# Paired loads, a regrouped triangular inverse and a new order table in phase two of a bidirectional RWKV-7 layer

## The chip, the cores and the metric

The kernel runs on one core of a Trainium2 chip. The metric is the device time of one execution in microseconds, taken as the median of several runs. The engines are named as in the profile: PE (TensorE, matmuls), ACT (ScalarE), DVE (VectorE), POOL (GpSimd) and SP (SyncE, which here only issues DMA transfers).

## What is computed

One layer of a bidirectional RWKV-7 trunk over 4096 + 512 tokens of width 1024 with 16 heads of 64: norm, input projection, a delta rule recurrence run forward and backward over the tokens, a group norm, gate, output projection and a last norm. The recurrence is what phase two of the kernel computes:

```python
def step(s, inp):
    r_t, w_t, k_t, v_t, kk_t, a_t = inp
    sa = jnp.einsum("bhvk,bhk->bhv", s, -kk_t)
    s = (s * w_t[:, :, None, :]
         + sa[..., None] * (kk_t * a_t)[:, :, None, :]
         + v_t[..., None] * k_t[:, :, None, :])
    return s, jnp.einsum("bhvk,bhk->bhv", s, r_t)
...
y_fwd = delta_rule_scan(r_h, heads(decay[:, :, 0]), ...)
y_bwd = flip(delta_rule_scan(flip(r_h), flip(heads(decay[:, :, 1])), ...))
y = y_fwd + y_bwd
```

## The kernel before

There are three phases: the input projection (to about 2000 us of the trace), the recurrence (to about 4290 us) and the output projection. The change touches the second alone.

Phase two does the recurrence in chunks of 64 tokens. A double step D covers 256 tokens of each direction (`tok` gives the first token: the forward direction goes up, the backward one down) for two pairs of heads, the halves `hf` 0 and 1, called lanes. There are 4 x 18 = 72 double steps. Each is cut into about 230 named steps. In a name the first figure is the half; in the names of four characters a second figure counts the chunk `i`.

- Loads, all on SP's queue, each issued in program order: `lk`, `lb`, `lr` (tiles `k`, `kb`, `r`, one transfer of 128 x 256 for each direction), `lt` (tile `ta`, L554, two transfers, one for each direction, each with both low-rank inputs x = 0 and 1), `uv` (values), `wa` (weights of the low-rank products, every 18th double step).
- Stage A: `lw` and `la` (L571, low-rank products of x = 0 and x = 1 on PE; both read `ta` and write `z`), tanh steps `tw`, `tW`, `ta`, `tA` on ACT, `pl`, the scan `sn` on DVE, exponentials `e1`, `e2`, then the elementwise steps `bf`, `al`, `kf`, `rh`, `kb`, `kk` on DVE (capital second letter: backward direction) with `fc` on ACT, scores `s0` to `s7` on PE with masks `m0` to `m3` on DVE, transposes `x0`, `x1` on PE with copies `c0`, `c1` on ACT.
- Triangular inverse of the 32 x 32 blocks: `ga` writes masked scores out to DRAM (eight transfers), `gw` and `gb` read them back as `w` and `lt`, then fifteen parts `E0` to `E14` (L783) run one after the other on the same tile `w`. Part b has the columns j = 2b+1 and 2b+2, each a product `tm` (or `td` on DVE) and an addition, of ceil(j/2) x (31-j) elements. `ON_DVE = (6, 12)` puts two parts on DVE, the others run on POOL. `ms` sets the diagonal on POOL, `S1` and `S2` move the result by DRAM into `xt`.
- Stage B: `xr`, `g0`, `g1`, `gc`, `gC`, `h0`, `h1`, `hc`, `hC` complete the inverse.
- Chain, four chunks for each lane: on PE `a` and `r` (into `py`), then a copy `q` to `rs` on ACT, `u` on PE (into `pr`), copies `v`, `V` to `uv` on ACT, `z` on PE, the state `w`, `W` on DVE after the decays `p`, `P` on ACT, and the output `y` on PE (into `py`), copied by `Y` and `Z` on ACT to `ys`; `yo` stores it.

The tiles `py` and `pr` are one PSUM bank for each lane, shared by `r` and `y`, and by `u` and `z`: instructions on one bank are kept in program order, reads against writes too.

Nothing is scheduled at run time. Every named step of every D has the key `D * PERIOD + ISSUE[name]`, with `PERIOD = 27.706`, and the steps are emitted in the order of these keys (L962 to L965). The numbers only set an order. On each engine and on SP's queue the instructions then run strictly in that order, and a step that waits holds up all behind it. `E6` of D is thus followed on POOL by `E7` of D, while PE works on the chain of an earlier D. `BURST` puts extra matmuls ahead of some steps at the start and end of the phase.

Of the kernel before, what the change touches and what calls it, by code (L numbers as in the profile page):

```python
# [19 lines left out]

PERIOD = 27.706

BURST = ((0, 'a00', 16), (69, 'g0', 5), (69, 'h0', 5), (69, 'u00', 5), (70, 'g0', 5), (70, 'h0', 5), (70, 'u00', 5), (71, 'g0', 5), (71, 'h0', 5), (71, 'u00', 5))

ON_DVE = (6, 12)
ACT_DECAY = 4
ISSUE = {
# [37 lines left out]
}  # L65
KT = DM // 128
NPAIR = 8
# [6 lines left out]
def kernel(  # L74
# [15 lines left out]
    def tt(eng, out, a, b, op=ALU.mult):  # L90
        eng.tensor_tensor(out=out, in0=a, in1=b, op=op)  # L91
# [379 lines left out]
    with ExitStack() as p2:  # L471
# [46 lines left out]
        def tok(D, d):  # L518
            q = D % NQ
            if q >= NQP:  # L520
                return LP + 256 * (q - NQP if d == 0 else NQ - 1 - q)
            return 256 * (q if d == 0 else NQP - 1 - q)
# [12 lines left out]
        def add(name, D, fn, *args):  # L535
            order.append((D * PERIOD + ISSUE[name], fn, args))

        st = {}
        wa_q = {}

# [2 lines left out]
            for n in range(2):  # L543
                nc.sync.dma_start(wa_q[g][n].rearrange("p d x f c -> p (d x f c)").bitcast(F32), lora_d[g, n].bitcast(F32))

        def load(D, hf, n, src):
            p = D // NQ * 2 + hf
            S = st.setdefault(D, {})
            x = lpool.tile([128, 2, 256], F32, tag=n, name=n, bufs=2 if n == "k2" else 1)
            for d in range(2):  # L550
                nc.sync.dma_start(x[:, d, :], src[128 * p:128 * (p + 1), tok(D, d):tok(D, d) + 256])
            S[n, hf] = x

        def load_ta(D):  # L554
            S = st.setdefault(D, {})
            S["ta"] = lpool.tile([128, 2, 2, 256], F32R, tag="ta", name="ta", bufs=1)
            for d in range(2):
                t0 = tok(D, d)
                nc.sync.dma_start(S["ta"][:, d].bitcast(F32), ta_d[d, :, :, t0:t0 + 256].rearrange("x p t -> p x t").bitcast(F32))

        def stage_a(D, hf):
            S = st[D]
# [41 lines left out]
            def bfac(d):  # L604
                if "ah" not in E:
                    E["ah"] = epool.tile([128, 2, 256], F32, tag="qw", name="ah")
                kb = S["kb", hf]
                stt(E["ah"][:, d, :], E["qa"][:, d, :], -1.0, kb[:, 0, :] if d == 0 else kb[:, 1, ::-1], ALU.add, ALU.mult)

            def facs(d):  # L610
                ACT.activation(E["qa"][:, d, :], E["qa"][:, d, :], AF.Identity, scale=ka_h[:, p:p + 1], bias=ka_1[:, p:p + 1])

            def alpha(d):
                k2 = S["k2", hf].rearrange("p d (i t) -> p d i t", t=64)
                stt(kept("ar", 2, 4, 128)[:, d, :, 0:64], k2[:, 0] if d == 0 else k2[:, 1, ::-1, ::-1], kkv[:, p:p + 1],
                    E["pp"][:, d, :, 0:64], ALU.mult, ALU.mult)

            def kfac(d):
                k2 = S["k2", hf]
                tt(DVE, k2[:, d, :], E["qa"][:, 0, :] if d == 0 else E["qa"][:, 1, ::-1], k2[:, d, :])  # L620

            def rho(d):
                r2 = S["r2", hf].rearrange("p d (i t) -> p d i t", t=64)
                pp = E["pp"]
                if d == 0:
                    tt(DVE, kept("ar", 2, 4, 128)[:, 0, :, 64:128], r2[:, 0], pp[:, 0, :, 1:65])
                else:
                    tt(DVE, kept("ar", 2, 4, 128)[:, 1, :, 64:128], r2[:, 1, ::-1, :], pp[:, 1, :, 64:0:-1])

            def ends():  # L630
                DVE.tensor_copy(out=kept("pt", 2, 4), in_=E["pp"][:, :, :, 64])
# [12 lines left out]
            def kap_k(d):  # L644
                bk = tile_bk()
                e8 = E["ee"]
                k8 = S["k2", hf].rearrange("p d (i t) -> p d i t", t=64)
                if d == 0:
                    tt(DVE, bk[:, 0, 64:576].rearrange("p (i x t) -> p i x t", x=2, t=64)[:, :, 1, :], k8[:, 0], e8[:, 0])
                else:  # L650
                    tt(DVE, bk[:, 1, 0:512].rearrange("p (i x t) -> p i x t", x=2, t=64)[:, :, 0, :],
                       k8[:, 1, ::-1, :], e8[:, 1, :, ::-1])

            def bk_(d, i):
                o = 128 * i + (64 if d == 0 else 0)
# [76 lines left out]
        def gather2(D):  # L732
            S = st[D]
            gd = S["gd"]
            lt = bpool.tile([128, 30, 32], F32, tag="lt", name="lt", bufs=2)
            for c in range(2):
                nc.sync.dma_start(lt[64 * c:64 * c + 64], gd.rearrange("u f h i b s t -> (u f h i b) s t")[:, 1:31])
            S["lt"] = lt

        def gather_w(D):  # L740
# [347 lines left out]
```

## Time and profile before

| | us |
|---|---|
| median of 3 runs | 4784.6 (4779.5 to 4804.6) |
| the profiled execution | 4773.8 |
| its span, first to last instruction | 4772.0 |
| PE busy in it | 4369.3 |
| DVE, ACT, POOL busy | 3437.4, 2866.8, 2608.6 |
| mean granted PE clock | 0.967 |

Durations are read from the one profiled execution, so a sum of them is set against its 4773.8 us. An engine's busy time is the sum over stages with different limits: in phase one PE does almost all, in phase two four engines are busy at about 74 to 89%. The idle time that a row shows in brackets is that of the engine just before the instruction, with what released it. PE's rows show the operand of a matmul as two or more instructions: `x4`, `x8` or `x16` is one or two of the named steps. The line tells the step: L576 `lw`/`la`, L664 `s`, L819 `g`, L833 `h`, L873 `a`, L878 `r`, L896 `u`, L905 `z`, L915 and L919 `y`.

### The profile page before, as it was taken

The numbers are of one execution on the slowest core, as the hardware profiler recorded it, in microseconds if no ns is written. First come the engines' busy times: TensorE is split into PE (matmuls) and PEld (weight loads), VectorE is DVE, ScalarE is ACT, GpSimd is POOL, SyncE is SP. The second block draws the span as 40 slices with busy tenths as digits, with TensorE's granted clock in tenths as the row PEclk, the third lists the DMA queues.
The fourth block names the chain that finished last, engine by engine and source line by source line (L and its number), as shares of the span: only waits on it lengthen the run. The fifth ranks groups of instructions, "written<-read, shape, count | busy, mean of one in ns | idle before, by whom it ended". The sixth has DMA issues, their size and how long they took to land.

```text
span 4772.0 us, 133366 instructions
## 1 busy us (share of the span) xinstructions
PE 4369.3 (92%) x52005; PEld 3842.4 (81%) x52005; DVE 3437.4 (72%) x6182; ACT 2866.8 (60%) x7355; POOL 2608.6 (55%) x4904
## 2 busy tenths in 40 slices
PE   8999999999999999688888888888888888886999
PEld 8999999999999999567777777777777777765887
DVE  6666666666665566677877877777787788747998
ACT  5454445444544444478777877777887787862332
POOL 2333333333333333377777767777776777744553
PEclk9999999999999999799999999999999999998999
DMA  4433333333333333466666656656666666638885
GB/s 133 154 110 115 105 120 110 115 106 119 110 115 109 99 102 105 121 153 150 146 159 154 158 134 154 160 140 151 158 157 156 147 157 153 157 78 269 269 267 187
DMA packets 1278855, 687.51 MB, mean 144 GB/s; under 512 B 665232, under 2 KB 1242768, under 8 KB 1278224
## 3 DMA queue, kind: packets, MB, share of 16 engines
q1 hardware_dynamic: 1278224, 678.99, 52.3%
q8 instruction: 409, 6.70, 0.6%
q14 instruction: 222, 1.82, 0.1%
HBM read 457.50 MB, written 221.25 MB: 142 GB/s over the span
## 4 chain that ended last, share of the span: by engine, by line
PE 63%; ACT 14%; DVE 7%; DMA 6%; issue 5%; POOL 2%; SPq 1%; ACTq 0%; DVEq 0%; POOLq 0%
PE acc L232 10%; PE acc L234 10%; PE acc L233 10%; PE acc L1039 8%; DMA ta<-ta_d 4%; ACT uv L899 3%; PE z L576 3%; PE py L915 3%; PE pr L896 3%; PE sp L664 3%; PE py L919 2%; PE py L878 2%; PE pr L905 2%; PE tp L673 2%; DMA r<-r_d 2%
## 5 line engine op out<-in xcount | busy, mean ns | idle before, releaser
L232 PE MATMUL acc<-hh,wh 128*128 128x384 f32 x3264 | 1108.1, 340 | 0.0
L234 PE MATMUL acc<-hh,wl 128*128 128x384 f32 x3264 | 1097.1, 336 | 0.0
L233 PE MATMUL acc<-hl,wh 128*128 128x384 f32 x3264 | 1096.3, 336 | 0.0
L91 POOL TENSOR_TENSOR tm<-lt,w 128x120 f32<-128x120 f32 (+7 forms) x1872 | 818.6, 437 | 486.8 <-DVE w L91 291.1
L91 POOL TENSOR_TENSOR w<-w,tm 128x120 f32<-128x120 f32 (+7 forms) x1872 | 838.3, 448 | 146.7
L232 PEld LDWEIGHTS acc<-hh,wh 128*128 128x128 f32 x3264 | 617.4, 189 | 0.2
L233 PEld LDWEIGHTS acc<-hl,wh 128*128 128x128 f32 x3264 | 617.3, 189 | 0.0
L234 PEld LDWEIGHTS acc<-hh,wl 128*128 128x128 f32 x3264 | 616.3, 189 | 0.0
L91 POOL TENSOR_TENSOR s<-u 128x384 f32<-128x384 f32 (+2 forms) x312 | 268.9, 862 | 603.4 <-ACT u L457 436.0
L94 DVE SCALAR_TENSOR_TENSOR sn<-pr,pt,sn 128x128 f32<-128x128 f32 x1152 | 356.1, 342 | 244.1 <-ACT sn L889 123.3
L889 ACT ACTIVATE sn<-sn,pt 128x128 f32<-128x128 f32 x1120 | 436.5, 397 | 40.5 <-PE py L915 34.4
L457 ACT ACTIVATE u<-acc 128x384 f32<-128x384 f32 x408 | 198.2, 486 | 353.6 <-PE acc L234 353.5
L91 DVE TENSOR_TENSOR sc<-sp,mask 128x512 f32<-128x512 f32 x576 | 372.3, 676 | 41.6 <-PE sp L664 40.7
L664 PE MATMUL sp<-ar,bk 64*128 64x128 f32 x4608 | 384.2, 296 | 8.2 <-DVE sc L91 6.4
L899 ACT ACTIVATE uv<-pr 64x128 f32<-64x128 f32 x1152 | 310.8, 270 | 68.9 <-PE pr L896 53.3
L664 PEld LDWEIGHTS sp<-ar,bk 64*128 64x128 f32 x4608 | 302.5, 192 | 61.5 <-issue 30.6
L915 PE MATMUL py<-sn,ar 128*64 128x128 f32 x2240 | 250.6, 304 | 97.5 <-ACT rs L882 97.5
L91 POOL TENSOR_TENSOR xl<-rk,xh 128x384 fp32r<-128x384 f32 (+1 forms) x96 | 97.5, 1016 | 428.1 <-ACT xh L264 428.1
L896 PE MATMUL pr<-rs,xt 64*64 64x64 f32 x4608 | 251.3, 235 | 48.6 <-ACT rs L882 48.6
L905 PE MATMUL pr<-uv,tb 128*64 128x64 f32 x4608 | 260.1, 236 | 35.9 <-ACT uv L899 35.7
L91 DVE TENSOR_TENSOR xl<-kq,xh 128x384 fp32r<-128x384 f32 (+1 forms) x96 | 93.4, 973 | 269.7 <-ACT xh L264 269.7
L91 DVE TENSOR_TENSOR wl<-wr,wh 128x1024 fp32r<-128x1024 f32 x136 | 182.8, 1344 | 137.0 <-ACT wh L223 136.8
(163 smaller groups left out, 9979.8 us busy)
## 6 DMA issues: line engine op xcount, KB each, us to landing
wr<-in_rw_in_dram SPq DMA_DIRECT2D x136, 512.0 KB, 4.2
ta<-ta_d SPq DMA_DIRECT2D x144, 256.0 KB, 4.6
k<-k_d SPq DMA_DIRECT2D x288, 128.0 KB, 3.8
kb<-kb_d SPq DMA_DIRECT2D x288, 128.0 KB, 3.2
r<-r_d SPq DMA_DIRECT2D x288, 128.0 KB, 3.3
uv<-v_d SPq DMA_DIRECT2D x288, 128.0 KB, 3.1
y_d<-ys SPq DMA_DIRECT2D x144, 256.0 KB, 3.2
lt<-gd SPq DMA_DIRECT2D x144, 240.0 KB, 4.3
```

The source lines that it names most:

```text
L91: eng.tensor_tensor(out=out, in0=a, in1=b, op=op)
L94: DVE.scalar_tensor_tensor(out=out, in0=a, scalar=s, in1=b, op0=op0, op1=op1)
L232: PE.matmul(ps, wh[:, k, :], hh[:, k, :], start=(k == 0), stop=False)
L233: PE.matmul(ps, wh[:, k, :], hl[:, k, :], start=False, stop=False)
L234: PE.matmul(ps, wl[:, k, :], hh[:, k, :], start=False, stop=(k == KT - 1))
L664: PE.matmul(E["sp", i2][h][:, d, j, :], bk_(d, i)[hs], ar[hs, d, i, :], start=True, stop=True)
L889: ACT.activation(o, before(i)[:, d, :], AF.Copy, scale=pt)
L896: PE.matmul(up[ua[d], hs], S["xt"][ua[d], 8 * hf + 4 * h + i, :], rs[ua[d], hs], start=True, stop=True)
L899: ACT.activation(S["uv", hf][ua[d], d, (i, 3 - i)[d], :], up[ua[d]], AF.Copy)
L905: PE.matmul(zp[hs, d, hs], S["tb", hf][:, d, i, hs], S["uv", hf][:, d, (i, 3 - i)[d], hs], start=True, stop=True)
L915: PE.matmul(o[d], S["ar", hf][:, d, i, 64:128], before(i)[:, d, :], start=True, stop=False)
L1039: PE.matmul(pn[n], a[:, k, :], w[:, k, 512 * n:512 * (n + 1)], start=first, stop=last)
```

## The change

Four things change in phase two.

1. `lk`, `lb`, `lr` load both directions by one transfer of 128 x 2 x 256: the lower start token, the distance to the other, and which half of the tile belongs to which direction. `lt` still has two transfers, but one for each x, with both directions in it. `gather2` reads the 30 rows of `lt` for both column halves by one transfer instead of two.
2. `ON_DVE` is (12, 13, 14) instead of (6, 12).
3. All numbers of `ISSUE` are new; `PERIOD` stays. 16 of the extra matmuls of `BURST` stand ahead of `gc` instead of `a00` of the first double step.
4. Steps that read `k`, `kb`, `r` take the half of their direction. `EWISE` and `ON_POOL` are new; as `ON_POOL` is empty, they leave every step on DVE.

```diff
-BURST = ((0, 'a00', 16), (69, 'g0', 5), ...
+BURST = ((0, 'gc', 16), (69, 'g0', 5), ...
-ON_DVE = (6, 12)
+ON_DVE = (12, 13, 14)
+
+ON_POOL = ()
 ISSUE = {
-    "wa": -2.9000, "lt": 0.0000, "lk0": 1.1591, "lw0": 1.2805, "lb0": 3.3493, "tw0": 7.3949, "tW0": 8.8003,
+    "wa": -2.9000, "lt": 0.0000, "lk0": 3.7346, "lw0": 4.3642, "tW0": 11.1877, "tw0": 11.4451, "lb0": 12.2391,
...
+        def EWISE(n):
+            return POOL if n in ON_POOL else DVE
...
+        def both(D):
+
+            t = [tok(D, d) for d in range(2)]
+            return min(t), abs(t[1] - t[0]), (0, 1) if t[0] < t[1] else (1, 0)
+
+        def strided(view, dims):
+            return bass.AP(tensor=view.tensor, offset=view.offset, ap=dims)
+
         def load(D, hf, n, src):
...
-            for d in range(2):
-                nc.sync.dma_start(x[:, d, :], src[128 * p:128 * (p + 1), tok(D, d):tok(D, d) + 256])
-            S[n, hf] = x
+            t0, gap, slot = both(D)
+            nc.sync.dma_start(x, strided(src[128 * p:128 * (p + 1), t0:t0 + 256], [[T, 128], [gap, 2], [1, 256]]))
+            S[n, hf] = [x[:, slot[d], :] for d in range(2)]
 
         def load_ta(D):
...
-            for d in range(2):
-                t0 = tok(D, d)
-                nc.sync.dma_start(S["ta"][:, d].bitcast(F32), ta_d[d, :, :, t0:t0 + 256].rearrange("x p t -> p x t").bitcast(F32))
+            t0, t1 = tok(D, 0), tok(D, 1)
+            for x in range(2):
+                src = strided(ta_d[0, x, :, t0:t0 + 256], [[T, 128], [256 * T + t1 - t0, 2], [1, 256]])
+                nc.sync.dma_start(S["ta"][:, :, x, :].bitcast(F32), src.bitcast(F32))
...
             def kfac(d):
-                k2 = S["k2", hf]
-                tt(DVE, k2[:, d, :], E["qa"][:, 0, :] if d == 0 else E["qa"][:, 1, ::-1], k2[:, d, :])
+                k2 = S["k2", hf][d]
+                tt(EWISE("kf"), k2, E["qa"][:, 0, :] if d == 0 else E["qa"][:, 1, ::-1], k2)
...
             lt = bpool.tile([128, 30, 32], F32, tag="lt", name="lt", bufs=2)
-            for c in range(2):
-                nc.sync.dma_start(lt[64 * c:64 * c + 64], gd.rearrange("u f h i b s t -> (u f h i b) s t")[:, 1:31])
+            nc.sync.dma_start(lt, strided(gd[0, 0, 0, 0, 0, 1:31, :], [[0, 2], [1024, 64], [1, 960]]))
             S["lt"] = lt
```

How the instructions then stand is shown at three places of a steady double step. First SP's queue, from the second half of `ga` to the store of `y`; the kernel before:

```order
L729 DMA gd<-sc 32x8x32 x4
L551 DMA r_39961<-r_d 128x256 x2
L551 DMA kb<-kb_d 128x256 x2
L801 DMA uv<-v_d 64x4x128 x2
L746 DMA w<-gd 64x16x32 x2
L737 DMA lt<-gd 64x960 x2
L551 DMA r_40191<-r_d 128x256 x2
L559 DMA ta<-ta_d 128x2x256 x2
L801 DMA uv<-v_d 64x4x128 x2
L551 DMA k_40253<-k_d 128x256 x2
L551 DMA kb<-kb_d 128x256 x2
```

and the changed kernel, at the same place:

```order
L745 DMA gd<-sc 32x8x32 x8
L566 DMA kb<-kb_d 128x2x256
L816 DMA uv<-v_d 64x4x128 x2
L752 DMA lt<-gd 128x1x960
L761 DMA w<-gd 64x16x32 x2
L575 DMA ta<-ta_d 128x2x256 x2
L566 DMA k_48969<-k_d 128x512
L566 DMA r_48981<-r_d 128x2x256
L954 DMA y_d<-ys 128x2x256 x2
L787 DMA wd<-w 1024x1x32 x2
L566 DMA kb<-kb_d 128x512
```

`ta` stood behind `w`, `lt` and the second `r`; it now stands behind `lt` and `w`, and `k` and `r` of the next loads follow it.

Next PE, from `z03` (the first row) to `lw`/`la` (`z<-ta`) and beyond; before, where the order is `z03`, `r13`, `y12`, `u13`, `a00`, `la1`, `x00`:

```order
L905 MATMUL pr0_19074<-uv_48752,tb_47400 64x64 x4
L878 MATMUL py1_19079<-sn_49622,ar_47525 64x128 x2
L915 MATMUL py1_19079<-sn_49536,ar_47525 64x128 x2
L919 MATMUL py1_19079<-uv_49182,sc_47779 64x64 x4
L896 MATMUL pr1_19077<-rs_49798,xt0_19095 64x64 x4
L873 MATMUL py0_19076<-uv_49362,sc_48066 64x64 x4
L576 MATMUL z_49826<-ta_49352,wah_39518 128x256
L576 MATMUL z_49826<-ta_49352,wal_39519 128x256
L576 MATMUL z_49826<-ta_49352,wah_39518 128x256
L576 MATMUL z_49826<-ta_49352,wal_39519 128x256
L673 MATMUL tp_49835<-ident_69,bk_49709 128x128 x4
```

and changed, where it is `z03`, `g0`, `g1`, `r13`, `la1`, `y12`, `a00`, `u13`:

```order
L920 MATMUL pr0_19074<-uv_48668,tb_47059 64x64 x4
L834 MATMUL iv2_49370<-x_49323,sc_47677 32x32 x16
L834 MATMUL iv2_49370<-x_49323,sc_48023 32x32 x16
L893 MATMUL py1_19079<-sn_49257,ar_47162 64x128 x2
L592 MATMUL z_49427<-ta_48911,wah_39191 128x256
L592 MATMUL z_49427<-ta_48911,wal_39192 128x256
L592 MATMUL z_49427<-ta_48911,wah_39191 128x256
L592 MATMUL z_49427<-ta_48911,wal_39192 128x256
L930 MATMUL py1_19079<-sn_49143,ar_47162 64x128 x2
L934 MATMUL py1_19079<-uv_48813,sc_47420 64x64 x4
L888 MATMUL py0_19076<-uv_49271,sc_47677 64x64 x4
L911 MATMUL pr1_19077<-rs_49438,xt0_19095 64x64 x4
```

`g0` and `g1` (`iv`) came behind `z03`, and `la1` moved from behind `a00` to between `r13` and `y12`.

Last ACT, around the copies `Z10` and `Y10` (`ys` from `py1`); before, where they stand ahead of the exponential (`pp`) and of `q12` and `q03` (`rs`):

```order
L925 ACTIVATE ys_44098<-py1_19079 128x128 x2
L596 ACTIVATE pp_44128<-d1_19099 128x520
L889 ACTIVATE sn_44132<-sn_44046,pt_42167 128x128
L925 ACTIVATE ys_44098<-py0_19076 128x128
L676 ACTIVATE tb_44161<-tp_44111 128x512
L882 ACTIVATE rs_44163<-py1_19079 128x128
L882 ACTIVATE rs_44165<-py0_19076 128x128
```

and changed, the rows after `q12`, `q03`, `Z00` and `e20`, down to `Y10` (the second `ys` from `py1`) and `Z01`:

```order
L914 ACTIVATE uv_50019<-pr1_19077 64x128 x2
L914 ACTIVATE uv_49874<-pr0_19074 64x128 x2
L627 ACTIVATE qa_50459<-qa_50459,ka_1_84,ka_h_83 128x256
L692 ACTIVATE tb_50408<-tp_50434 128x512
L599 ACTIVATE qw_50556<-z_50519,w0v1_80 128x256
L599 ACTIVATE qw_50556<-z_50519,w0v0_79 128x256
L940 ACTIVATE ys_50493<-py1_19079 128x128
L627 ACTIVATE qa_50459<-qa_50459,ka_1_84,ka_h_83 128x256
L904 ACTIVATE sn_50576<-sn_50427,pt_48257 128x128
L940 ACTIVATE ys_50493<-py1_19079 128x128
L940 ACTIVATE ys_50493<-py0_19076 128x128
```

Both copies from `py1` moved from ahead of `q12` to far behind it, and `c01` (`tb`) no longer stands between them and the copies to `rs`.

## Rows read from the trace of the kernel before

**Rows 1.** The page's section 1: busy us, share of the span, instructions

```profile
PE 4369.3 (92%) x52005; PEld 3842.4 (81%) x52005; DVE 3437.4 (72%) x6182; ACT 2866.8 (60%) x7355; POOL 2608.6 (55%) x4904
```

**Rows 2.** Windows of phase two: busy us (instructions), PEclk, DMA share, GB/s

```profile
2200.00:4100.00 1900.00, 1693.31 (x32756) 1353.98 (x32752) 1485.49 (x3547) 1501.90 (x4451) 1401.52 (x3250) 0.97 0.63 153
...
3390.00:3512.00 122.00, 108.77 (x2162) 86.84 (x2158) 98.66 (x236) 99.03 (x295) 91.91 (x215) 1.00 0.65 155
...
3818.70:3940.50 121.80, 109.59 (x2204) 87.96 (x2204) 101.28 (x238) 100.19 (x298) 92.22 (x221) 1.00 0.65 157
...
2966.00:2981.00 15.00, 13.79 (x156) 11.17 (x158) 8.67 (x22) 7.33 (x23) 11.02 (x30) 0.54 0.52 120
```

**Rows 3.** Chain of work that ended last, by line, from 2200 to 4100 us

```profile
by line: DMA ta<-ta_d 8.9%; ACT uv L899 6.7%; PE z L576 6.6%; PE pr L896 5.9%; PE py L915 5.9%; PE sp L664 4.9%; PE py L919 4.8%; PE py L878 4.7%; PE pr L905 4.6%; DMA r<-r_d 4.3%; issue 4.3%; PE tp L673 4.2%; ACT rs L882 3.9%; PE iv L819 3
```

**Rows 4.** Timeline of PE, one period: start, us, instruction, idle before it

```profile
2871.21 0.45 PE L905 MATMUL pr<-uv,tb 128*64 128x64 f32 x8 [0.25 <-ACT uv L899]
...
2873.62 0.39 PE L576 MATMUL z<-ta,wah 128*128 128x256 f32 x1 [0.73 <-DMA ta<-ta_d]
...
2875.16 0.44 PE L915 MATMUL py<-sn,ar 128*64 128x128 f32 x4 [0.44 <-ACT rs L882]
...
2876.86 0.45 PE L905 MATMUL pr<-uv,tb 128*64 128x64 f32 x8 [0.26 <-ACT uv L899]
...
2879.12 0.44 PE L915 MATMUL py<-sn,ar 128*64 128x128 f32 x4 [0.44 <-ACT rs L882]
...
2886.72 0.68 PE L896 MATMUL pr<-rs,xt 64*64 64x64 f32 x16 [0.68 <-ACT rs L882]
...
2892.88 0.44 PE L915 MATMUL py<-sn,ar 128*64 128x128 f32 x4 [0.46 <-ACT rs L882]
```

**Rows 5.** Timeline of PE, same columns: ends of two pieces of a period

```profile
2868.79 0.94 PE L664 MATMUL sp<-ar,bk 64*128 64x128 f32 x12
...
2872.39 0.39 PE L576 MATMUL z<-ta,wah 128*128 128x256 f32 x1
...
2890.62 1.20 PE L819 MATMUL iv<-x,sc 32*32 32x32 f32 x64
...
2894.34 0.28 PE L576 MATMUL z<-ta,wal 128*128 128x256 f32 x1
...
2903.42 0.39 PE L576 MATMUL z<-ta,wah 128*128 128x256 f32 x1
```

**Rows 6.** Timeline of PE: first and last of nine long waits for ta

```profile
2299.42 0.39 PE L576 MATMUL z<-ta,wah 128*128 128x256 f32 x1 [1.49 <-DMA ta<-ta_d]
...
4163.41 0.39 PE L576 MATMUL z<-ta,wah 128*128 128x256 f32 x1 [0.84 <-DMA ta<-ta_d]
```

**Rows 7.** Timeline of the SP queue: start of issue, its us, transfers

```profile
2893.65 1.27 SPq L746 DMA_DIRECT2D w<-gd  x2
...
2896.59 1.01 SPq L551 DMA_DIRECT2D r<-r_d  x2
...
2897.70 0.89 SPq L559 DMA_DIRECT2D ta<-ta_d  x2
```

**Rows 8.** DMA issues, 2200 to 4100: count, KB each, us to landing

```profile
ta<-ta_d SPq DMA_DIRECT2D x122, 256.0 KB, 4.7
...
r<-r_d SPq DMA_DIRECT2D x241, 128.0 KB, 3.5
```

**Rows 9.** Waits, 2200 to 4100: us in total, times, longest

```profile
POOL tm L91 <- DVE w L91: 247.8, 118, 7.4
...
ACT ys L925 <- PE py L878: 124.9, 60, 3.5
...
DVE ar L91 <- DMA r<-r_d: 115.8, 50, 5.8
```

**Rows 10.** Groups by shape, 2200 to 4100: busy us, mean ns, idle

```profile
L591 DVE TENSOR_TENSOR_SCAN d<-smask,d 128x520 f32<-128x520 bf16 x120 | 156.4, 1303 | 55.9 <-ACT d L586 55.9
...
L91 DVE TENSOR_TENSOR td<-lt,w 128x126 f32<-128x126 f32 x60 | 16.2, 270 | 0.0
```

More of the change, by code (lines that the diff above doesn't have):

```diff
@@ L21 @@
 PERIOD = 27.706
-BURST = ((0, 'a00', 16), (69, 'g0', 5), (69, 'h0', 5), (69, 'u00', 5), (70, 'g0', 5), (70, 'h0', 5), (70, 'u00', 5), (71, 'g0', 5), (71, 'h0', 5), (71, 'u00', 5))
-ON_DVE = (6, 12)
+BURST = ((0, 'gc', 16), (69, 'g0', 5), (69, 'h0', 5), (69, 'u00', 5), (70, 'g0', 5), (70, 'h0', 5), (70, 'u00', 5), (71, 'g0', 5), (71, 'h0', 5), (71, 'u00', 5))
 ACT_DECAY = 4
+ON_DVE = (12, 13, 14)
+ON_POOL = ()
 ISSUE = {
[37 rows of a table removed]
[38 rows of a table added]
 }
@@ L607, in bfac @@
                 kb = S["kb", hf]
-                stt(E["ah"][:, d, :], E["qa"][:, d, :], -1.0, kb[:, 0, :] if d == 0 else kb[:, 1, ::-1], ALU.add, ALU.mult)
+                stt(E["ah"][:, d, :], E["qa"][:, d, :], -1.0, kb[0] if d == 0 else kb[1][:, ::-1], ALU.add, ALU.mult)
             def facs(d):
@@ L613, in alpha @@
             def alpha(d):
-                k2 = S["k2", hf].rearrange("p d (i t) -> p d i t", t=64)
-                stt(kept("ar", 2, 4, 128)[:, d, :, 0:64], k2[:, 0] if d == 0 else k2[:, 1, ::-1, ::-1], kkv[:, p:p + 1],
+                k2 = S["k2", hf][d].rearrange("p (i t) -> p i t", t=64)
+                stt(kept("ar", 2, 4, 128)[:, d, :, 0:64], k2 if d == 0 else k2[:, ::-1, ::-1], kkv[:, p:p + 1],
                     E["pp"][:, d, :, 0:64], ALU.mult, ALU.mult)
             def kfac(d):
-                k2 = S["k2", hf]
-                tt(DVE, k2[:, d, :], E["qa"][:, 0, :] if d == 0 else E["qa"][:, 1, ::-1], k2[:, d, :])
+                k2 = S["k2", hf][d]
+                tt(EWISE("kf"), k2, E["qa"][:, 0, :] if d == 0 else E["qa"][:, 1, ::-1], k2)
             def rho(d):
-                r2 = S["r2", hf].rearrange("p d (i t) -> p d i t", t=64)
+                r2 = S["r2", hf][d].rearrange("p (i t) -> p i t", t=64)
                 pp = E["pp"]
                 if d == 0:
-                    tt(DVE, kept("ar", 2, 4, 128)[:, 0, :, 64:128], r2[:, 0], pp[:, 0, :, 1:65])
+                    tt(EWISE("rh"), kept("ar", 2, 4, 128)[:, 0, :, 64:128], r2, pp[:, 0, :, 1:65])
                 else:
-                    tt(DVE, kept("ar", 2, 4, 128)[:, 1, :, 64:128], r2[:, 1, ::-1, :], pp[:, 1, :, 64:0:-1])
+                    tt(EWISE("rh"), kept("ar", 2, 4, 128)[:, 1, :, 64:128], r2[:, ::-1, :], pp[:, 1, :, 64:0:-1])
             def ends():
@@ L646, in kap_k @@
                 e8 = E["ee"]
-                k8 = S["k2", hf].rearrange("p d (i t) -> p d i t", t=64)
+                k8 = S["k2", hf][d].rearrange("p (i t) -> p i t", t=64)
                 if d == 0:
-                    tt(DVE, bk[:, 0, 64:576].rearrange("p (i x t) -> p i x t", x=2, t=64)[:, :, 1, :], k8[:, 0], e8[:, 0])
+                    tt(EWISE("kk"), bk[:, 0, 64:576].rearrange("p (i x t) -> p i x t", x=2, t=64)[:, :, 1, :], k8, e8[:, 0])
                 else:
-                    tt(DVE, bk[:, 1, 0:512].rearrange("p (i x t) -> p i x t", x=2, t=64)[:, :, 0, :],
-                       k8[:, 1, ::-1, :], e8[:, 1, :, ::-1])
+                    tt(EWISE("kk"), bk[:, 1, 0:512].rearrange("p (i x t) -> p i x t", x=2, t=64)[:, :, 0, :],
+                       k8[:, ::-1, :], e8[:, 1, :, ::-1])
             def bk_(d, i):
```

73 rows, old and new, of the table ISSUE are left out of this document.

## The prediction

> **What bounds the kernel now.** I read the page's head first: every engine is busy over half of the span, so no share settles anything [rows 1]. The change touches phase two alone, so I went to the stretch from 2200 to 4100 us. The scan runs twice per double step D and 120 times here [rows 10]: 60 double steps in 1900 us, **31.7 us each**, 72 in all. PE is busy 1693 us of 1900, ACT 1502, DVE 1485 and POOL 1402 [rows 2]: PE is nearest to the bound, and still idle 3.4 us per step. In two stretches at the full clock the same work is faster: 2162 + 2204 PE instructions at 32756/60 = 546 per step are 8.0 steps in 243.8 us, **30.5 us each** [rows 2]. The missing 1.2 us is the clock. [...] The chain of waits agrees that loads matter: `ta` 8.9% and `r` 4.3%, the rest nearly all PE and ACT handing over to each other [rows 3].
>
> So a step costs 30.5 us of lockstep plus some 1.1 us of low clock. In a clean step PE waits seven times, 3.26 us together [rows 4]: for `ta` 0.73; three times for the copy `q` before a `y` (0.44, 0.44, 0.46); before `u12` 0.68; before `z00` and `z01` 0.25 and 0.26.
>
> **The loads.** Six pairs of transfers become six transfers, and `lt<-gd` two become one: seven of 38 issues fall away on SP. A pair took 0.9 to 1.0 us to issue, and one `ta` transfer, of the merged shape, 0.89/2 = 0.45 [rows 7], so SP gains about 3 us per step. That is no time by itself; what counts is when `ta` and `r` land. Now `ta` is issued after `r`, which waits for `rho` on DVE, and lands about when PE asks. PE asks 2903.42 - 2894.34 = 9.1 us after the last `la1` matmul began, 8.8 after its end [rows 5]; the issue was at 2897.70 [rows 7], 3.1 us after that end, the second transfer goes out 0.45 later and landing takes 4.7 at the median [rows 8]: 8.2 to 8.3, a margin of 0.5 us, which any slower landing uses up. In the new order `ta` stands ahead of `r` and directly behind `w`, and its first transfer holds x = 0 of both directions, all that `lw0` reads. `uv1`, `lt` and `w` must be issued after `z03`: `w` takes 1.27 [rows 7], `uv1` I put at the same and `lt` at half, 3.2 us. Meanwhile PE runs `g0`, `g1` (1.2 [rows 5]), `r13` and `la1` (about 1). So `ta` is issued some 1.1 us after `la1`, and x = 0 lands 4.7 later, at 5.8. PE now asks sooner. From `s70` to `lw0` were 2872.39 - 2868.79 = 3.6 us [rows 5], of which only `s40` (0.3) stays between; `y12`, `a00` and `u13` come in, 1.3 us: 8.8 - 3.3 + 1.3 = 6.8 us. The margin grows from 0.5 to 1.0 us, and by as much again if the new PE waits below come first. I take the 0.73 as gone.
>
> `r` cost DVE 115.8 us, 1.9 per step [rows 9]. It is still issued after `rho` of the other half; but five DVE instructions (2.1 us at the mean of 0.42, 1485/3547 [rows 2]) now stand between `rho` and `rH1` that stood elsewhere. Against that, rows price the merging: 256 KB lands in 4.7 us, 128 KB in 3.5 [rows 8], so the merged `r` lands 0.75 us later than the second of two at 0.45 distance. I take the wait as gone, worth nothing on PE directly. [...]
>
> **The inverse.** Block 6 (126 and 119 elements) goes from DVE to POOL; 13 and 14 (56, 42, 30, 15) go to DVE. DVE loses four instructions of 0.27 and gains eight of at most 0.27 [rows 10]: +0.6 to +1.0 us of 24.8. POOL loses four of 0.43 (1402/3250 [rows 2]): -1.7 us. Today POOL waits 247.8 us for DVE in 118 handovers, 4.1 us per step [rows 9], yet DVE never waits for POOL there; now one handover goes over and `ms` waits for `E14`, three blocks into the next chain. POOL's 23.4 us busy leave room. I cost the move at nothing while POOL stays ahead; without that cover `w`, `xt` and `u` would come late by the shortfall. The DVE microseconds I count below.
>
> **The order on PE and ACT.** Step by step, from [rows 4]:
> - `y` after `r`: the new table puts `y00`, `y01`, `y10`, `y11` and `y12` ahead of the copy `q`, so PE does not wait; `u`, one step later, waits for a copy that starts a `y` later. Saved 1.34, cost 3 x 0.1.
> - `u12`: its copy stood behind `Y10`, which waits 2.1 us for `r12` [rows 9], then an exponential, `Z00` and `c01`. Only `Y00` is left: 0.68 becomes 0.1.
> - `z00`: `V00`, `P00`, `fC1`, `v00` stand in this order on ACT, two instructions (0.34 each by the mean, 1502/4451 [rows 2]) between the copies; one score step (0.3) comes in on PE: 0.25 becomes 0.6. `z01`: 0.26 becomes 0.
> - New: `Y10` reads the bank that `r13` writes and now stands before it, the 15th instruction on ACT after `q12`: 15 x 0.34 + 0.3 = 5.4 us after that copy began. PE gets from `u12` to `y12` in 2892.88 - 2886.72 = 6.2 us [rows 4], 0.65 of it waits; without the transposition that moved (0.5) and with `r13` before `y12` it reaches `r13` 4.6 us after `u12`, 5.0 after `q12`. Wait 0.4, between 0 and 1.1.
> - New: `W13`, for which `r10` waits, stands behind `bf1`, `al1` and `aL1`, 3 x 0.42 = 1.3 us, while `lw0` (0.6) comes ahead of `r10` on PE: up to 0.7 late, I take 0.4, between 0 and 1.0.
> - New: `a10` behind `Y11`: 0.1.
>
> PE's waits become 0.3 + 0.1 + 0.6 + 0.4 + 0.4 + 0.1 = 1.9 for 3.26: 1.36 us less. I let two thirds through, **0.9 us**, since DVE carries 0.6 to 1.0 more and both it and ACT stand at 78%. Bounds: nothing, and the 1.36.
>
> **Sum** against the profiled execution, 4773.8 us (span 4772.0 and 1.8 around it): 72 x 0.9 = -65. Low clock: of 57 to 72 us, nine of fourteen stretches hang on `ta`; I take -30, between 0 and -60. Once, a deeper pipeline: the last key moves from 142.4 to 148.9, at 30.5/27.7 about +7. Together -88: 4686. The median of the runs stands 10.8 us above the profiled execution, so **4697 us**.
>
> **Rivals.**
> - A, the lockstep does not care: ACT or DVE take back what PE stops waiting for, as a gain elsewhere has no claim on PE. Then 0 to 0.3 us per step (22 us) and 0 to 30 of the low clock are left: 4784.6 + 7 less 0 to 52, **4740 to 4792**. For it: DVE loses 1.9 us to `r` today and PE hardly notices in a clean step.
> - B, slower, by the clock: nine stretches followed PE waits of 0.76 to 3.82 us. `r13` and `r10` put two new waits of 0.4 to 1.1 us into every step. A low stretch costs 72/14 = 5 us. Beyond (65 - 7)/5 + 14, some 26 of 72 steps, the clock eats the gain; with one in every second step more than today it is 4784.6 - 65 + 7 + 36 x 5 - 72 = **4835**. Against it: the sum of PE's waits falls. [...]
> - C, slower, by VectorE: its new 0.6 to 1.0 us land ahead of `W13`, `W00` and `W10`, for which `r10`, `r01` and `r11` wait. At 1 us per step beyond what the order saves: 4784.6 + 72 - 30 + 7 = **4834**. Decides from 1.4 us of extra DVE lateness per step.
> - That the change does not do what it says: the built program shows the seven issues gone and `lw0` waiting for one transfer; I give it nothing.
>
> **How the numbers follow.** Forecast 0.52 (4640 to 4745), A 0.28, B 0.12, C 0.08. Measurement tells 0.5% (24 us) from no change: faster is below 4761, slower above 4808. A falls half on either side of 4761. Faster 0.66, same 0.16, slower 0.18. The range keeps the forecast's own and A whole and leaves out most of B and C: 4635 to 4795.
>
> **What would show it.** Right: a clean step of 29.5 to 29.8 us; no PE wait for `ta` in the ordinary step and fewer low stretches; `r` gone from DVE's waits; POOL's wait for DVE under 1 us per step; a wait of about 0.4 us before `r13` on ACT's `ys`. Wrong: PE's idle stays 3.4 us with other names (A), PEclk falls below 0.96 over the stretch (B), or PE waits on DVE before `r` for 1 us and more (C).

## The result and the profile after

The changed kernel takes **5324.7 us** (median of 4 runs, 5317 to 5333) against 4782.0 for the kernel before on the same chip (4 runs): ratio 1.1137, 95% interval 1.1078 to 1.1197. I had forecast 4697 within 4635 to 4795; it is 543 us slower instead of 88 faster. The profiled execution is of 5324.5 us.

The head of the page of the changed kernel (busy us, share of the span and instructions; then 40 slices, the granted clock in tenths):

```profile
PE 4565.1 (86%) x52005; PEld 4028.3 (76%) x52005; DVE 3486.7 (66%) x6470; ACT 2884.5 (54%) x7355; POOL 2413.9 (45%) x4616
...
PEclk9999999999999987878878787787887887887999
```

Against [rows 1] the engines have about the same work; PE's 196 us more are the same 52005 instructions at a lower clock (a mean of 0.886 granted, 0.967 before). From the start of phase two the granted clock of a slice alternates between 0.7 and 0.8. Windows of the changed kernel, columns as in [rows 2]:

```profile
2200.00:4100.00 1900.00, 1499.69 (x26262) 1218.63 (x26262) 1224.63 (x3039) 1221.39 (x3577) 990.02 (x2412) 0.81 0.49 123
3612.00:3627.60 15.60, 14.39 (x307) 12.04 (x305) 14.12 (x30) 13.79 (x44) 13.56 (x27) 0.98 0.66 145
3628.40:3635.70 7.30, 6.74 (x152) 5.45 (x149) 6.23 (x15) 6.55 (x18) 1.46 (x4) 1.00 0.24 65
3635.70:3639.00 3.30, 0.00 (x0) 0.00 (x0) 0.00 (x0) 0.78 (x2) 0.00 (x0) 0.63 0.35 83
3639.00:3651.00 12.00, 9.13 (x98) 7.22 (x100) 4.68 (x20) 4.51 (x14) 5.76 (x20) 0.53 0.53 148
```

The scan runs 97 times in the first row: 48.5 double steps, **39.2 us each** instead of 31.7. The four rows under it follow one step. It starts healthy; then POOL has almost nothing to do and the DMA engines fall to 0.24 busy and 65 GB/s, while the other engines still have work; then for 3.3 us no compute engine but ACT does anything; then PE works at 0.53 of the clock, nearly all of it at a lower level of half the full clock: a window from 3640 to 3650 us has 0.50. What SP and PE did there (SP's queue as in [rows 7], PE as in [rows 4]):

```profile
3627.06 0.52 SPq L752 DMA_DIRECT2D lt<-gd  x1
3627.63 8.05 SPq L761 DMA_DIRECT2D w<-gd  x2
3635.72 3.98 SPq L575 DMA_DIRECT2D ta<-ta_d  x2
3639.80 0.41 SPq L566 DMA_DIRECT2D k<-k_d  x1
3640.31 0.38 SPq L566 DMA_DIRECT2D r<-r_d  x1
```

```profile
3641.68 0.58 PE L592 MATMUL z<-ta,wah 128*128 128x256 f32 x1 [6.21 <-DMA ta<-ta_d]
```

The merged `lt` goes out in 0.52 us, and then SP's issues stall: the two `w` take 8.05 us instead of 1.27 and the two `ta` 3.98 instead of 0.89 [rows 7]; the medians over 2200 to 4100 us are 8.03 and 4.03. The second `ta` is out some 10 us later than with the times of [rows 7], PE stands for 6.21 us, and the granted clock is at the lower level from within this wait on (0.50 from 3637 to 3639 us). The waits over 2200 to 4100 us, where `r` had cost DVE 115.8 us [rows 9] and `ta` had cost PE this (the kernel before, same view):

```profile
PE z L576 <- DMA ta<-ta_d: 27.0, 44, 3.8
```

and the changed kernel:

```profile
POOL tm L95 <- DMA w<-gd: 559.7, 48, 16.9
DVE ar L95 <- DMA r<-r_d: 514.5, 48, 15.3
ACT rs L897 <- PE py L893: 384.9, 92, 12.7
PE z L592 <- DMA ta<-ta_d: 331.7, 48, 11.8
```

One wait for each in every step. Why the DMA engines are idle meanwhile shows in the packets of `lt`, the only ones of 3840 bytes. Before, the 128 packets of a step were gone in 2.46 us (median), 11.0 of them under way on average. Now they take **10.45 us with 2.0 under way**. A single packet is no slower: 0.15 us at the median, 0.22 before. The landings tell the same. A load of phase two gives its semaphore sixteen updates in the trace, and each merged `lt` three: in the step above at 3628.03, 3639.25 and 3639.41, one right behind the issue and two behind the last packet. Which of the 16 DMA engines carry these packets the trace does not tell. The source of the load was written as `[[0, 2], [1024, 64], [1, 960]]`: the rows read twice, and the slowest dimension is that 2.

### The profile page after: what moved, and what is told of

Same layout as the page of the kernel before. It is cut to its first block, busy times and chain, and to the rows that moved or that the text cites. A ratio compares the mean times of both kernels' runs of the same rounds, so it can differ in the third digit from the quotient of the medians.

```text
span 5322.8 us, 133076 instructions
## 1 busy us (share of the span) xinstructions
PE 4565.1 (86%) x52005; PEld 4028.3 (76%) x52005; DVE 3486.7 (66%) x6470; ACT 2884.5 (54%) x7355; POOL 2413.9 (45%) x4616
## 2 busy tenths in 40 slices
DMA packets 1257492, 687.46 MB, mean 129 GB/s; under 512 B 656160, under 2 KB 1209120, under 8 KB 1256864
## 5 line engine op out<-in xcount | busy, mean ns | idle before, releaser
L95 POOL TENSOR_TENSOR tm<-lt,w 128x110 f32<-128x110 f32 (+3 forms) x1728 | 719.7, 416 | 999.6 <-DMA w<-gd 869.7
L95 POOL TENSOR_TENSOR w<-w,tm 128x110 f32<-128x110 f32 (+3 forms) x1728 | 740.8, 429 | 135.4 <-POOL tm L95 0.2
L592 PE MATMUL z<-ta,wah 128*128 128x256 f32 x576 | 208.5, 378 | 504.3 <-DMA ta<-ta_d 484.9
L897 ACT ACTIVATE rs<-py 128x128 f32<-128x128 f32 x576 | 159.8, 277 | 875.4 <-PE py L893 547.7
L95 DVE TENSOR_TENSOR ar<-r,pp 128x256 f32<-128x256 f32 x288 | 138.2, 480 | 754.6 <-DMA r<-r_d 754.6
L592 PEld LDWEIGHTS z<-ta,wah 128*128 128x128 f32 x576 | 127.1, 221 | 541.9 <-DMA ta<-ta_d 447.6
L680 PE MATMUL sp<-ar,bk 64*128 64x128 f32 x4608 | 461.5, 329 | 1.6 <-DVE sc L95 1.6
L680 PEld LDWEIGHTS sp<-ar,bk 64*128 64x128 f32 x4608 | 344.8, 212 | 53.9 <-issue 15.0
L893 PE MATMUL py<-sn,ar 128*64 128x128 f32 x2240 | 289.9, 345 | 58.4 <-ACT ys L940 45.6
L911 PE MATMUL pr<-rs,xt 64*64 64x64 f32 x4608 | 307.1, 265 | 18.5 <-ACT rs L897 8.4
```

What stands on the lines that cost most here:

```text
L592: PE.matmul(z[:, d, :], w[:, d, x, hf, :], S["ta"][:, d, x, :], start=(n == 0), stop=(n == 1))
L680: PE.matmul(E["sp", i2][h][:, d, j, :], bk_(d, i)[hs], ar[hs, d, i, :], start=True, stop=True)
L893: PE.matmul(rp[ua[d], :], S["ar", hf][:, d, i, 0:64], before(i)[:, d, :], start=False, stop=True)
L911: PE.matmul(up[ua[d], hs], S["xt"][ua[d], 8 * hf + 4 * h + i, :], rs[ua[d], hs], start=True, stop=True)
```

## The experiments

The kernel before ran beside each set, with medians of 4818.1 (E1 to E4), 4811.9 (E5 to E8) and 4818.7 us (E9 to E12); its chips differ by nearly 1%, so kernels of different sets are compared by their ratios.

| kernel | us | ratio to before | 95% interval |
|---|---|---|---|
| changed | 5324.7 | 1.1137 | 1.1078 to 1.1197 |
| E1 changed, `lt` in two | 4829.6 | 1.0024 | 1.0013 to 1.0036 |
| E2 before, `lt` merged | 5525.6 | 1.1482 | 1.1458 to 1.1506 |
| E3 before, other loads merged | 4785.7 | 0.9942 | 0.9924 to 0.9960 |
| E4 E1, old blocks on DVE | 5097.2 | 1.0589 | 1.0572 to 1.0606 |
| E5 E1, `r` loaded earlier | 4798.5 | 0.9973 | 0.9951 to 0.9995 |
| E6 E1, `rho` later | **4648.6** | 0.9663 | 0.9628 to 0.9697 |
| E7 E5, copies moved | 4811.7 | 1.0004 | 0.9982 to 1.0026 |
| E8 changed, `lt` as 62 + 2 rows | 5427.6 | 1.1279 | 1.1239 to 1.1319 |
| E9 E6, old blocks on DVE | 5018.9 | 1.0424 | 1.0373 to 1.0475 |
| E10 E6, copies moved | **4618.1** | 0.9583 | 0.9529 to 0.9637 |
| E11 E6, no load merged | 4835.0 | 1.0026 | 0.9995 to 1.0057 |
| E12 before, `rho` later | 4786.8 | 0.9944 | 0.9915 to 0.9972 |

### The loss: E1, E2, E8

E1 takes the merged `lt` back:

```diff
-            nc.sync.dma_start(lt, strided(gd[0, 0, 0, 0, 0, 1:31, :], [[0, 2], [1024, 64], [1, 960]]))
+            for c in range(2):
+                nc.sync.dma_start(lt[64 * c:64 * c + 64], gd.rearrange("u f h i b s t -> (u f h i b) s t")[:, 1:31])
```

> The changed kernel with one edit: `lt<-gd` is again two transfers of 64 rows, as in the kernel before; everything else of the change stays. Theory L (the one merged `lt` transfer is the whole loss): in the changed kernel the DMA engines are 0.24 busy at 65 GB/s in the 7.3 us after its issue, SP's next transfers take 7.2 and 3.6 us to issue instead of about 0.6, `w` and `ta` come late, PE waits some 6 us for `ta` in every double step and falls to the lower clock. With two transfers that goes away and what I had forecast for the rest stands: 4697 us, between 4640 and 4745, no wait for `w` on POOL beyond 1 us, PE's wait for `ta` under 0.3 us per step. [...] Rival T (the new order itself loses, and the late `w` is a symptom): the time stays above 5000 us, and PE keeps waiting 3 us or more per step for something else.

Measured 1.0024. The one transfer is worth 0.111 of 4782 us, 532 of the 543 us lost: theory L holds for the loss. What it said of the rest does not: 4697 would have been 0.982, and E1 is no faster than before; nor did POOL's wait for `w` go under 1 us (4.7 us in each of 37 waits).

E2 is the kernel before with the merged load alone:

```diff
-            for c in range(2):
-                nc.sync.dma_start(lt[64 * c:64 * c + 64], gd.rearrange("u f h i b s t -> (u f h i b) s t")[:, 1:31])
+            nc.sync.dma_start(lt, bass.AP(tensor=gd.tensor, offset=gd[0, 0, 0, 0, 0, 1:31, :].offset, ap=[[0, 2], [1024, 64], [1, 960]]))
```

> The kernel before with one edit: `lt<-gd` is one transfer of 128 rows, as in the changed kernel; order, blocks and loads stay old. Theory L: the transfer takes about 10.5 us instead of 2.4 and SP's queue stands still behind it for some 8 to 11 us. In the old order `w` goes out ahead of it, but the second `r` and `ta` go out behind it: `ta` lands about 8 us later against a margin of 0.5 us, so PE loses 6 us or more in every one of 72 steps, and the lower clock follows: 5150 to 5450 us. Rival T: the cost of the merged transfer needs the new order, in which it stands ahead of `w`; here it is hidden, and the time stays within 2% of 4782.

Measured 1.148, above the range, and the rival is out: the line needs no new order to do harm. Here `w` is out already, and `r` and `ta` are what stands behind (E2, SP's queue, then its waits):

```profile
3444.38 0.54 SPq L736 DMA_DIRECT2D lt<-gd  x1
3445.02 1.13 SPq L551 DMA_DIRECT2D r<-r_d  x2
3446.25 3.60 SPq L559 DMA_DIRECT2D ta<-ta_d  x2
```

```profile
DVE ar L91 <- DMA r<-r_d: 497.8, 50, 14.8
...
PE z L576 <- DMA ta<-ta_d: 336.1, 45, 11.4
```

E8 merges nothing, and only counts the rows otherwise:

```diff
-            nc.sync.dma_start(lt, strided(gd[0, 0, 0, 0, 0, 1:31, :], [[0, 2], [1024, 64], [1, 960]]))
+            for c in range(2):
+                for a, b in ((0, 62), (62, 64)):
+                    nc.sync.dma_start(lt[64 * c + a:64 * c + b], gd.rearrange("u f h i b s t -> (u f h i b) s t")[a:b, 1:31])
```

> Changed kernel, `lt<-gd` in four transfers: for each half of 64 rows one of 62 rows and one of 2. Nothing is merged here; only the number of rows per transfer differs from 64. Theory L in its sharper form (how many engines a transfer gets depends on the length of its slowest dimension, and merging harmed only because that dimension became 2): the load is on two engines again, SP stands still as in the changed kernel, 5200 to 5400 us. [...] Rival (the harm came from one large transfer of 480 KB, or from reading every row twice): four small transfers are as good as two, about 4830 to 4860 us.

Measured 5427.6, like the changed kernel and a little worse, with 1.95 packets of `lt` under way, 11.6 us for them, and three updates of the semaphore for each of the four transfers (E8, SP's queue):

```profile
3410.99 1.34 SPq L754 DMA_DIRECT2D lt<-gd  x4
3412.38 7.64 SPq L763 DMA_DIRECT2D w<-gd  x2
3420.12 4.66 SPq L575 DMA_DIRECT2D ta<-ta_d  x2
```

So neither the size of the transfer nor the double read was needed for the harm. What goes with it is the length of the slowest dimension: with 64 rows 11.0 packets were under way and a transfer gave its semaphore sixteen updates, with the doubled source 2.0 and three, with 62 and 2 rows 1.95 and three. That 62 rows would not spread either was my expectation and came true; why they do not is not shown.

### Where the forecast gain went: E5, E6, E7

E1's trace has the answer. Its windows row, some of its waits, then one step on SP, DVE and PE:

```profile
2200.00:4100.00 1900.00, 1658.81 (x31842) 1357.38 (x31840) 1498.88 (x3693) 1479.75 (x4332) 1204.66 (x2928) 0.94 0.62 149
```

```profile
DVE ar L95 <- DMA r<-r_d: 224.8, 59, 7.5
POOL w L780 <- DVE td L95: 210.1, 59, 5.0
POOL tm L95 <- DMA w<-gd: 175.4, 37, 8.0
...
PE py L894 <- DVE sn L98: 102.6, 56, 3.6
...
PE z L592 <- DMA ta<-ta_d: 16.8, 19, 3.7
```

```profile
3500.62 1.98 SPq L575 DMA_DIRECT2D ta<-ta_d  x2
3502.70 0.41 SPq L566 DMA_DIRECT2D k<-k_d  x1
3503.22 0.54 SPq L566 DMA_DIRECT2D r<-r_d  x1
```

```profile
3509.51 0.43 DVE L95 TENSOR_TENSOR ar<-r,pp 128x256 f32<-128x256 f32 x1 [5.51 <-DMA r<-r_d]
```

```profile
3512.77 0.69 PE L894 MATMUL py<-sn,ar 128*64 128x128 f32 x4 [3.38 <-DVE sn L98]
```

With 117 scans a step is 32.5 us. `ta` is nearly cured (16.8 us), but the two `ta` directly behind `lt` and `w` take 1.98 us to issue (2.32 at the median of 59 steps, 0.89 before), and `r` stands behind them. It then lands 6.3 us after its issue in this step, 4.9 at the median, where the two smaller `r` of the kernel before took 3.5 [rows 8]. DVE waits for it in every step, 3.8 us on average, at `rH1`; behind `rH1` stand `E12`, `E13`, `rh1` and then `W00`, for which PE's `r01` waits 1.8 us per step. The clock falls more often too: 46 low stretches between 2150 and 4200 us, 15 by the same count in the kernel before. E5 moves the load:

```diff
-    "lr1": 31.7879,
+    "lr1": 25.4500,
```

> Changed kernel, `lt` in two transfers, and one number more: `lr1` (the load of `r` for the second half) goes out between `gb` and `gw` instead of behind `w`, `ta` and `k`. In the kernel with `lt` in two transfers VectorE waits 224.8 us in 59 waits for `r` (3.8 per step), with `E12`, `E13`, `rh1` and then `W00` queued behind `rH1`, and PE waits 102.6 us in 56 waits for the state ahead of `r` (1.8 per step); the low stretches of the clock begin there (46 of them). Theory R (the late `r` eats the forecast gain): SP issues this transfer about 6 us earlier, the wait for `r` falls under 1 us per step, PE's wait for the state under 0.4, low stretches to 15 or fewer: 4620 to 4720 us. Rival A (lockstep): the wait moves elsewhere and the time stays within 1% of the kernel with `lt` in two transfers (about 4830). Cost on the other side: `w` and `ta` go out 0.6 us later.

E6 moves the reader:

```diff
-    "rH1": 32.7455, "rh1": 33.8886,
+    "rH1": 36.9000, "rh1": 36.9200,
```

> Changed kernel, `lt` in two transfers, and instead of the load the reader is moved: `rH1` and `rh1` stand behind `w10` on VectorE, so that `E12` to `E14`, `W00`, `w00`, `W10` and `w10` no longer stand behind the wait for `r`. Theory R: PE's wait for the state ahead of `r` goes (1.8 us per step), VectorE's wait for `r` falls below 1 us as the reader stands some 4 us later; 4620 to 4740 us. If only the lateness of `r` itself counted, because its product is needed at once, PE would wait at the scores instead and the time would stay at about 4830.

E5 misses its range by 78 us; rival A's 1% holds. The wait for `r` is gone as forecast, and another has its place (E5, waits over the same stretch):

```profile
PE z L592 <- DMA ta<-ta_d: 91.3, 55, 5.1
...
DVE ar L95 <- DMA r<-r_d: 9.3, 6, 3.3
```

The lateness moved from `r` to `ta`, which now has `r` ahead of it as well. E6 leaves the queue alone and has 4648.6 us, in its range and 3.6% below E1:

```profile
2200.00:4100.00 1900.00, 1722.18 (x34712) 1406.85 (x34711) 1672.41 (x4005) 1599.75 (x4710) 1318.99 (x3186) 0.99 0.66 161
```

```profile
3469.23 0.44 PE L894 MATMUL py<-sn,ar 128*64 128x128 f32 x4 [0.59 <-ACT ys L941]
...
3480.50 0.45 PE L921 MATMUL pr<-uv,tb 128*64 128x64 f32 x8 [0.73 <-ACT uv L915]
...
3498.40 0.44 PE L894 MATMUL py<-sn,ar 128*64 128x128 f32 x4 [0.66 <-ACT ys L941]
```

126 scans are 30.2 us per step; from `r13` to the next `r13` 29.17 us pass in a clean step; 7 low stretches are left. No wait of DVE for `r` is left among its rows, though the two `ta` still take 2.39 us to issue (median) and `r` still lands 4.6 us after its issue. The late `r` had done its harm by what was queued behind its reader.

E7 is E5 with the two waits taken away that the rows of E6 above still show:

```diff
-    "v00": 116.7054, "Z10": 132.1801, "Y10": 132.7804,
+    "v00": 116.0500, "Z10": 129.2990, "Y10": 129.2995,
```

> As the kernel with `lr1` early, and the two waits on ACT that I had forecast are taken away: `Z10` and `Y10` stand directly behind `Z00` (ahead of `e20`, `v12`) and `v00` ahead of `P00`. Theory (my terms): PE's waits before `r13` (0.66 us in the trace of the kernel with `lt` in two transfers) and before `z00` (0.73) fall to 0.2 or less together, worth 0.5 to 1.0 us per step, 35 to 70 us against the kernel with `lr1` early. Rival A: ACT gives the time back elsewhere (`v12` and `V12` now start 0.6 us later), and the difference is under 15 us.

1.0004 against 0.9973: no gain, rival A. PE waited for `ta` there anyway, 115.2 us over the stretch after 91.3 in E5.

### The terms one by one: E3, E4, E9, E10, E11, E12

E3 is the kernel before with the changed `load` and `load_ta`, and the readers that go with them; `lt`, table and blocks are old:

```diff
-            for d in range(2):
-                nc.sync.dma_start(x[:, d, :], src[128 * p:128 * (p + 1), tok(D, d):tok(D, d) + 256])
+            t0, gap, slot = both(D)
+            nc.sync.dma_start(x, strided(src[128 * p:128 * (p + 1), t0:t0 + 256], [[T, 128], [gap, 2], [1, 256]]))
...
-            for d in range(2):
...
+            for x in range(2):
```

> The kernel before with the other merged loads alone: `k`, `kb`, `r` in one transfer for both directions, `ta` in one for each x; `lt` stays two transfers, the order and the blocks on VectorE stay old. Theory (my terms): SP has six issues less and `lw0` waits for one transfer instead of two, so PE's wait for `ta` falls from 0.5 to 1 us per step to about half and some low clock with it; `r` of 256 KB lands 0.75 us later than by two, which PE does not feel: 4730 to 4785 us. Rival: 256 KB transfers land so much later that `ta` and `r` are late, 4800 us or more.

0.9942, 28 us, at the edge of the range. PE's wait for `ta` goes from 27.0 to 21.6 us, not to half; `r` stays (116.3 after 115.8). Where the 28 us come from is not shown.

E4 and E9 undo the move of the blocks in E1 and in E6:

```diff
-ON_DVE = (12, 13, 14)
+ON_DVE = (6, 12)
```

> As the first of these (changed kernel, `lt` in two transfers), and blocks 6 and 12 of the triangular inverse on VectorE as before instead of 12, 13 and 14. Theory (my term): the move is worth nothing on the path, since POOL has room; POOL waits for VectorE again some 4 us per step, and the time is within 0.5% (24 us) of the kernel with `lt` in two transfers. Rival: in the new order POOL is late without the move, and the time is 40 us or more above that kernel; or VectorE is the tighter engine, and it is 40 us or more below.

> The kernel with `rH1` and `rh1` late (4648.6 us, `lt` in two transfers), and blocks 6 and 12 on VectorE as before instead of 12, 13 and 14. Theory (my term): the move is worth nothing on the path as long as nothing else makes VectorE wait, so the loss of 267 us that the same edit cost in the order with the early `rH1` was the wait for `r` again, handed on by block 6: within 0.5% (23 us) of 4648. Rival: POOL is late without the move in this order, also without a wait for `r`: 4750 us or more.

Both far above 0.5%: 1.0589 against 1.0024, 1.0424 against 0.9663. In the new order block 6 stands on DVE behind the elementwise steps of another double step, and the inverse changes hands with a wait each way (E9, waits, 54 steps in the stretch):

```profile
POOL tm L95 <- DVE w L95: 535.4, 108, 12.4
DVE td L95 <- POOL w L95: 260.6, 54, 5.1
...
PE z L592 <- DMA ta<-ta_d: 162.4, 52, 6.4
...
DVE ar L95 <- DMA r<-r_d: 41.3, 30, 3.2
```

POOL waits 9.9 us per step, where the order before had 4.1 [rows 9]. DVE's wait for `r` is only 0.8 us per step in E9, against 7.4 in E4, so it is not `r` that block 6 hands on, and the rival is right there: POOL is late. PE also waits 3.0 us per step for `ta`; whether that follows from the late POOL or adds to it was not tried.

E10 is E6 with the diff of E7.

> The kernel with `rH1` and `rh1` late, and `Z10` and `Y10` directly behind `Z00`, `v00` ahead of `P00` on ACT. In its trace PE waits 0.59 to 0.66 us before `r13` and 0.73 before `z00` in each clean step of 29.1 us, the two waits that I had forecast at 0.4 and 0.6. Theory (waits of PE add up): both fall under 0.2, 0.5 to 1.1 us per step: 4570 to 4615 us. Rival A (lockstep): the time stays within 15 us of 4648.

4618.1 us, 30 us less than E6 by the medians and just above the range; the intervals of the two ratios still touch, so a gain is likely and not shown. The waits moved in part: `r13` and `z00` fall from 84.3 us over 1900 to 0.7, and PE now waits 53.5 us for ACT's `ys` ahead of `a` (L889), with 38.3 for `ta` instead of 23.0. E10 and E6 beat both kernels; E10 is the fastest measured.

E11 is E6 with each load in two transfers, as before, `ta` one for each direction; in the terms of E3's diff:

```diff
-            nc.sync.dma_start(x, strided(src[128 * p:128 * (p + 1), t0:t0 + 256], [[T, 128], [gap, 2], [1, 256]]))
+            for d in range(2):
+                nc.sync.dma_start(x[:, d, :], src[128 * p:128 * (p + 1), tok(D, d):tok(D, d) + 256])
```

> The kernel with `rH1` and `rh1` late, and every load in two transfers as in the kernel before, `ta` one for each direction: the new order and blocks alone, without any merging. Theory (my term): merging saves SP some 3 us per step and puts x = 0 of `ta` into the first transfer, so without it `ta` and `r` land 1 to 2 us later, PE waits for `ta` again in most steps and the clock falls: 4680 to 4780 us. Rival: the merged loads are worth nothing in this order: within 0.5% of 4648.

1.0026, above the range: all of E6's gain is gone. Merging is worth 28 us in the old order and about 174 in the new one (0.0363 of 4800). E11's waits, 59 steps, where E6 has 156.0 us in 38 waits for `w` and 23.0 for `ta`:

```profile
POOL tm L92 <- DMA w<-gd: 333.3, 59, 8.7
...
PE z L577 <- DMA ta<-ta_d: 87.2, 85, 4.8
```

E12 moves the reader in the kernel before, behind `w10`:

```diff
-    "rH1": 27.7889, "rh1": 30.5646,
+    "rH1": 32.7000, "rh1": 32.7200,
```

> The kernel before with `rH1` and `rh1` behind `w10` on VectorE, nothing else. There VectorE waits 115.8 us in 50 waits for `r` (1.9 per step of 60) and `W00` to `w10` stand behind. Theory (mine at the forecast): PE hardly notices that wait in the old order, 4760 to 4815 us, within 0.5% of before. Rival: the wait for `r` was already what held the old order, and moving the reader gives most of the gain there too: 4700 us or less.

0.9944, in the range by time and just over 0.5% by the ratio: DVE's wait for `r` falls from 115.8 to 1.9 us and PE gets little of it. The late reader decides only in the new order.

## Why the prediction was wrong

- **The bound before** was read rightly as far as E6 can tell, which has two edits that the forecast did not have: with the wait for `r` gone and 23.0 us left for `ta`, a clean step takes 29.2 us (forecast 29.5 to 29.8), the granted clock is 0.99, and there are 7 low stretches for 15. That its 4648.6 us lie within my range is no hit: the gain is 0.034 of the time where I had forecast 0.018, and it needs the moved reader. Two readings were off by one: I counted 14 of these 15, and the period of [rows 4] has an eighth wait of PE, 0.19 us at 2890.14. Neither is where the forecast failed. The 57 to 72 us of low clock in my sum are 0.03 x 1900 and (31.7 - 30.5) x 60 [rows 2]; that 30 of them hang on `ta` no run shows. E6's 0.99, with the wait for `r` gone as well, leaves 0.01 x 1900 = 19 us.
- **The step that failed is "`lt` at half".** I priced the merged `lt` by its issue, 0.52 us as it turned out, and never asked how it would be carried. Only its landing matters, and everything behind it on SP. A row against it could not stand in the trace, since no load of phase two had such a source before. An estimate from the packets of the trace before, with two at a time as the changed kernel then showed (2.0): 128 of them take 9.6 us at the 0.15 us of the quicker ones and 14 at the median of 0.22. The runs show what the line costs: 10.45 us for the data of `lt` instead of 2.46, and the two `ta` issued some 10 us later, against the margin of 0.5 to 1.0 us that I had worked out for `ta`.
- **`r` "gone, worth nothing on PE"** failed too, and E6 shows that it ate what I had forecast: in E1 the wait is 3.8 us per step on DVE and 1.8 on PE. I counted five DVE instructions of room, and took SP's issue of `ta` at 0.89 us as in [rows 7]; behind `lt` and `w` it is 2.32 at the median (E1). And I never looked behind `rH1` on DVE: `W00` stands there. That is rival C's place with another price, a wait in place of added work, and rival B's clock behind it: E1 has 46 low stretches.
- **`ta`** moved the way that was forecast once `lt` was split, but was not gone: 0.29 us per step in E1 (16.8 in 58.5) and 0.37 in E6 (23.0 in 63) for 0.45 (27.0 in 60).
- **The blocks "at nothing"**: mis-sized. The sum was not hurt, since the move is in it either way, but the reason, room on POOL, was wrong: without the move the new order loses 270 to 370 us (E4, E9). The sign that I had named, POOL's wait for DVE under 1 us per step, did not come either: 3.6 us in E1 (210.1 in 58.5), before `ms`, and 1.3 in E6.
- **The waits on ACT** were right: `r13` 0.66 us (41.4 in 63) for 0.4 within 0 to 1.1, `z00` 0.68 (42.9 in 63) for 0.6. The 0.4 for `r10` did not show. What their removal is worth (E10) is not settled.
- **The range** left out the truth because every rival was a mechanism of the order. That a new form of transfer might be carried otherwise than its neighbours had no chance at all.

## What to carry to other kernels

Before two transfers are merged, write down the access pattern and read its slowest dimension: 64 rows went out 11 packets at a time, a leading 2 went out two at a time, and everything behind it on the queue paid. When a load is late, look at what is queued behind its reader on the reader's engine; moving the reader behind that work gave 3.6%, moving the load up gave 0.5% and shifted the wait to the next load. An order table is bound to the loads and the division of work that it was made for: a part that is worth 0.6% in one order was worth 3.6% in another.

## What the runs showed of the hardware

The same issue on SP did not always take the same time: two `ta` took 0.89 us behind `r` [rows 7], 2.32 at the median behind `lt` and `w` in E1, and two `w`, 1.27 us in [rows 7], took 8.03 behind the merged `lt` with its 2.0 packets under way, with no semaphore that the profile shows. In the step shown above `lt` landed at 3639.41, and SP issues in 0.4 us again from 3639.80 on. What SP waits for until then the runs do not show, and why `ta` takes longer in E1 stays open. And a slow load need not be seen as busy DMA engines: the changed kernel moves the same bytes (687.46 MB, 687.51 before), and while POOL waits for what is queued behind one load they are 0.24 busy (3628.40 to 3635.70 us).
